# Attention by head pairs: scores on alternating row halves of the array, value products as unsplit float32 on its column halves

## The chip, the core and the metric

The kernel runs on one core of a Trainium2 chip. The metric is device time in microseconds (us), the median of three runs. The engines are named as in the profile: PE is TensorE's matmul, PEld its weight load, DVE is VectorE, ACT is ScalarE, POOL is GpSimd, SP is SyncE.

## The reference

Two layers of an encoder on 512 tokens of width 1024. A layer normalises its input, projects it, and feeds three head groups: A, six heads of dense latent attention; B, six heads of dilated window attention; C, a state-space layer. Their outputs are normalised, concatenated, projected and added to the input; a gated MLP with a convolution follows. What the change touches are the two attentions, cut here to their core:

```python
def dense_attention(q, k, v):                       # group A, head size 96 for q and k, 64 for v
    sc = einsum("bhqe,bhke->bhqk", qb, k) * e ** -0.5
    p = softmax(sc, axis=-1)
    return einsum("bhqk,bhkd->bhqd", p, v)

def dilated_branch(q, k, v, window, dilation):      # group B, head size 64, three patterns
    sc = where(valid, einsum("bhrnqe,bhrnke->bhrnqk", qb, kb) * e ** -0.5, NEG_INF)
    p = exp(sc - max(sc)); den = sum(p)
    o = einsum("bhrnqk,bhrnke->bhrnqe", p, vb) / den   # branches merged by their denominators
```

## The kernel before, in words

The input projection, the state-space layer, attention, the output projection (tile wo) and the MLP (tiles up and dn) run one after the other, for layer 0 and then layer 1. Products are made in float32r, a form of float32 that the array takes in one pass with less precision; to keep precision an operand is split into a high part (ACT rounds it) and a low part (DVE or POOL subtracts), and a product is three matmuls: high by high, low by high, high by low (`mm3`, L348 to L350). The transposes and the small sums are plain float32.

Attention (in `mixing`, from L995) works in heads, two heads to a pair. Group B's three pairs come first, then group A's three. The two heads of a B pair lie on partitions 0-63 and 64-127 of the same tiles; an A head fills 128 rows. For each head, `scores` makes a 128-query tile against 512 keys by three matmuls into a bank of tag sc: 64 rows of the array for B, 128 for A. `unit` then makes the softmax: DVE scales, adds the mask and takes the minimum (L1068, tile P), ACT takes the exponential (L1070), PE transposes P in four blocks into a bank of tag pt (L1074), ACT copies that as the high part (pth, L1078), and DVE makes the low part (ptl, L1079). After two such tiles, `pv` multiplies them with the values: per block of 128 keys three matmuls of 256 columns (L1086 to L1088), twelve for each head and each half of the queries. All of them write 128 partitions, as the values of a head are padded with 64 columns of zeros (`values`, `vput`, tiles vah, val, vbh, vbl), so that the two heads of a pair add into one bank of tag pv. `finish_pair` divides by the sums.

Between these, other work of the layer is traced at lower priority: queries and keys of later heads (`dil_qk` for B, `mla_qk` for A; the latter queues its root and its key's last steps in `later`, which `catch_up` runs), the gated output of group C (`s5_glu`), the norms of the three groups (`mix_group`) and A's values (`mla_values`). In layer 0, `background` also brings in chunks of the modulation (a load and one long DVE instruction each). A scheduler orders every engine's instructions when the kernel is built: by priority, `low(name)` sets it back or ahead, `after` puts instructions behind another one on the same engine. The order on an engine is then fixed. PSUM has eight banks; in attention three go to side work (ps), one to pv, two to pt, two to sc. Heads of A are made ahead: the queries and keys of head h + 3 are traced after the units of head h, into three sets of buffers (`qk_parts`).

Of the kernel before, what the change touches and what calls it, by code (L numbers as in the profile page):

```python
# [28 lines left out]
MB = (1, 1)  # L29
# [41 lines left out]
def _constants():  # L71
# [44 lines left out]
    # angle per position and sign of the sine  # L116
# [100 lines left out]
def program(ctx, tc, a, out):  # L217
# [9 lines left out]
    # 16 tiles: the normed input in two parts, then group A's latents (0-7) and two pairs of queries and keys (8-15)  # L227
# [147 lines left out]
    def bcast42(r4):  # L375
        """r4 [128 tokens, 4, 2] -> PSUM [128, 512]: the first value on partitions 0-63, the second above."""
# [8 lines left out]
    def row_rsqrt(parts, root=False, nt=4):  # L385
        """parts: (maker of a tile AP [rows, 512] of squares, weight column AP [rows, 1]); -> rsqrt(sum + eps) [128, 4]."""
# [18 lines left out]
    def x_norm(c, first):  # L405
        """1 / root mean square of the tokens c of x, on every partition; first: of the kernel's input."""
# [22 lines left out]
    def scaled(l, which, gname):  # L429
        """gain * (1 + sc) columns and the shift columns of one sub-layer."""  # L430
# [14 lines left out]
    def norm_half(l, which, g, c):  # L445
        """which: 0 before the mixing, 24 before the gated MLP. In steps: squares, sums, broadcast, the normed input."""
# [8 lines left out]
    def step(gen, ins):  # L455
        """the next step of a norm, on the tensor engine behind ins; gives its last instruction there."""
# [9 lines left out]
    def rope_tables():  # L466
# [5 lines left out]
        for tab, f in ((tabA, fr[:, 0:1]), (tabS, fr[:, 3:4])):  # L472
            # the angle less whole turns
# [8 lines left out]
            # cosines as sin(pi/2 - |x|)  # L482
# [33 lines left out]
        # rotation tables exp(i*4*theta*n), n ascending forwards, descending backwards  # L516
# [3 lines left out]
        # powers of the discretised diagonal, exponents -2..2  # L520
# [14 lines left out]
        # (a_bar - 1) / a  # L535
# [212 lines left out]
    def mixing(l, background):  # L748
# [5 lines left out]
        # x normed, shifted and scaled, split in two parts  # L754
# [24 lines left out]
        # input projection  # L779
# [17 lines left out]
        def proj_halves(o):  # L797
            """the first group of columns, its first half in one half of the tokens after the other"""
# [48 lines left out]
        def qk_parts(name, src, par):  # L847
            if par:
                i = 4 + 4 * par + 2 * (name == "k")
                hi, lo = ht(i), ht(i + 1)  # L850
            else:
                hi, lo = (mp.tile([128, N], F32R, tag=f"{name}{x}0", name=name + x) for x in "hl")
# [24 lines left out]
        # group C's channels and group B  # L877
# [52 lines left out]
        # group A latents: their mean squares  # L930
# [8 lines left out]
        # ra: columns (cq, ckv) x 4 token tiles; extra: mean-square share of the rotary key + eps  # L939
# [28 lines left out]
        # the 64 rows that are left: the high part, and the low part under it  # L968
# [5 lines left out]
        # roped key part, on rows 64-95 and again on 96-127  # L974
# [5 lines left out]
        # over the latent's factor, which the keys' common one brings back  # L980
# [16 lines left out]
        banks(f"pb{l}", att, ps=3, pv=1, pt=2, sc=2)  # L997
# [5 lines left out]
        # small weights of group A  # L1003
# [39 lines left out]
        def values(name):  # L1043
            hi = ap.tile([128, 4, 576], F32R, tag="vh", name=name + "h")
            lo = ap.tile([128, 4, 576], F32R, tag="vl", name=name + "l")
            for v in (hi, lo):
                G.memset(as32(v).rearrange("p t (c k) -> p (t c) k", k=192)[:, :, 64:128], 0.0)
            return hi, lo

        def vput(vh, vl, t, src, r):  # L1050
            """src PSUM [128 tokens, 384] (times r per token) into the padded layout, two parts."""
            s6 = src.rearrange("p (c k) -> p c k", k=128)
            h6, l6 = (v[:, t].rearrange("p (c k) -> p c k", k=192) for v in (vh, vl))
            for i in range(2):
                si, o = s6[:, :, i * 64:i * 64 + 64], slice(i * 128, i * 128 + 64)
                S.activation(h6[:, :, o], si, AF.Identity, scale=1.0 if r is None else r)
                if r is None:
                    V.tensor_tensor(l6[:, :, o], si, as32(h6[:, :, o]), sub)
                else:
                    V.scalar_tensor_tensor(l6[:, :, o], si, r, as32(h6[:, :, o]), mul, sub)  # L1060

        zero = zcol.to_broadcast([128, N])

        def unit(S_ps, scale, qt, PT, sums, pre):
            """softmax of one 128-query tile, transposed into PT (two parts); scale: minus the scores' factor."""
# [10 lines left out]
            ph, pl = PT  # L1076
            qc = slice(qt % 2 * 128, qt % 2 * 128 + 128)
            S.copy(ph[:, :, qc], t3)  # L1078
            V.tensor_tensor(pl[:, :, qc], t3, as32(ph[:, :, qc]), sub)  # L1079

        def pv(o, PT, vh, vl, hh, first, last, pr):
            c0 = pr * 192 + hh * 64
            ph, pl = PT
            for k in range(4):
                vhk, vlk = vh[:, k, c0:c0 + 128], vl[:, k, c0:c0 + 128]
                T.matmul(o, vhk, ph[:, k], start=(first and k == 0), stop=False)  # L1086
                T.matmul(o, vlk, ph[:, k], start=False, stop=False)  # L1087
                T.matmul(o, vhk, pl[:, k], start=False, stop=(last and k == 3))  # L1088

        def pt_tiles():  # L1090
            return (ap.tile([128, 4, 256], F32R, tag="pth", name="pth", bufs=2),
                    ap.tile([128, 4, 256], F32R, tag="ptl", name="ptl", bufs=2))
# [9 lines left out]
        def scores(q, k, rows, qt):  # L1102
            o = ps("sc", "sc")
            c = slice(qt * 128, qt * 128 + 128)
            (qh, ql), (kh, kl) = q, k
            T.matmul(o, qh[rows, c], kh[rows], start=True, stop=False)  # L1106
            T.matmul(o, ql[rows, c], kh[rows], start=False, stop=False)  # L1107
            T.matmul(o, qh[rows, c], kl[rows], start=False, stop=True)  # L1108
            return o

        full = slice(0, 128)
# [3 lines left out]
        def mla_qk(h, wq):  # L1115
# [18 lines left out]
            q = qk_parts("q", qf, h % 3)  # L1134
            made = [q, None, None]

            def roots():
# [18 lines left out]
                def rest():  # L1156
# [3 lines left out]
                    made[1] = qk_parts("k", kf, h % 3)  # L1160
# [6 lines left out]
        def mla_values():  # L1167
            wuv = small(a["w_uv"][l], 384, name="wuv")
            vh, vl = values("va")
            for t in range(4):  # L1170
# [5 lines left out]
                vput(vh, vl, t, o[:, :384], ra[:, 4 + t:5 + t])  # L1176
            return vh, vl
# [11 lines left out]
        # group B: the three branches as one softmax with key multiplicities  # L1189
        with low("vb"):  # L1190
          dvh, dvl = values("vb")
          for t in range(4):
            o = ps("vtp")
            for j in range(3):
                T.transpose(o[:, j * 128:(j + 1) * 128], draw[6 + j][:, t * 128:t * 128 + 128], ident)
            vput(dvh, dvl, t, o[:, :384], None)
        for pr in range(3):
            q, k = ahead[pr]
            sums = ap.tile([128, 8], F32, tag="sums", name="sums", bufs=2)
            o = ps("pv", "pv")  # L1200
            for hh in range(2):
                rows = slice(hh * 64, hh * 64 + 64)
                for half in range(2):
                    PT = pt_tiles()
                    for qt in (2 * half, 2 * half + 1):
                        unit(scores(q, k, rows, qt), -0.125, qt, PT,
                             sums[:, hh * 4 + qt:hh * 4 + qt + 1], K("bias", 384 - 128 * qt, 512))
                    with low("pv"):
                        pv(o[:, half * 256:half * 256 + 256], PT, dvh, dvl, hh, hh + half == 0, hh + half == 2, pr)
                    catch_up()  # L1210
                    if pr == 0 and hh == half:
                        with low("dq"):
# [286 lines left out]
```

## Time and profile before

| | us |
|---|---|
| median of 3 runs | 1524.69 (1522.24 to 1528.4) |
| the profiled execution, its span from the first instruction to the last | 1525.1 |
| PE busy in it | 1422.6 (93%) |
| DVE busy | 1092.1 (72%) |
| ACT busy | 721.4 (47%) |
| POOL busy | 380.2 (25%) |

The page gives no other time of the profiled execution than its span; nothing around it is shown. A busy matmul time is a union of modelled durations, which run past the start of the next matmul; how long one really holds the array is seen from the distance between the starts of two that follow each other. An fp32r tile prints as f32 among a matmul's operands, so the type is read from the code. A float32 product that is not a transpose stands as two matmuls in the trace.

### The profile page before, as it was taken

Reading aid. Unit: us, or ns where it says so; the run is one execution under the profiler, and the core shown is the slowest. Engines: PE = TensorE matmul, PEld = TensorE weight load, DVE = VectorE, ACT = ScalarE, POOL = GpSimd, SP = SyncE. Lnnn points to the kernel's source line nnn. Section 1 sums busy time; section 2 is a strip of 40 time slices with the busy share of each in tenths; the row PEclk is TensorE's granted clock in tenths of the full one; section 3 lists DMA queues with packets and bytes.
Section 4 is the critical chain, followed back from the end, with each engine's and each line's share of the span. In section 5 each row is a group of like instructions: output and inputs, shape, how many; then the busy total and the mean of one; then the engine's idle time right before and its main releaser. Section 6 shows DMA issues by size and latency. Waiting matters only on the chain.

```text
span 1525.1 us, 20842 instructions
## 1 busy us (share of the span) xinstructions
PE 1422.6 (93%) x7352; PEld 1177.7 (77%) x7352; DVE 1092.1 (72%) x2189; ACT 721.4 (47%) x1419; POOL 380.2 (25%) x330
## 2 busy tenths in 40 slices
PE   4879789989889999999998979999999999999998
PEld 3658567768878878888888867678898888888887
DVE  7996976886799789788656387758748663664663
ACT  4464265675354434444456324657635442442441
POOL 2566441231122153233233334313202000000000
PEclk9989888899999999999999889989999999999999
DMA  7665312311748467467336342000031333233332
GB/s 252 193 190 183 120 27 76 92 36 51 224 146 262 125 222 249 147 218 241 106 100 198 105 130 65 24 27 10 1 104 61 101 102 100 88 95 106 91 93 98
DMA packets 79115, 185.14 MB, mean 121 GB/s; under 512 B 12705, under 2 KB 37793, under 8 KB 79010
## 3 DMA queue, kind: packets, MB, share of 16 engines
q1 hardware_dynamic: 77712, 181.43, 38.0%
q10 hardware_dynamic: 1298, 2.37, 0.4%
q8 instruction: 58, 0.95, 0.3%
q14 instruction: 47, 0.39, 0.1%
HBM read 165.95 MB, written 15.73 MB: 119 GB/s over the span
## 4 chain that ended last, share of the span: by engine, by line
PE 67%; DVE 11%; ACT 3%; issue 3%; DMA 3%; POOL 2%; DVEq 0%; ACTq 0%; POOLq 0%; SPq 0%
PE up L349 10%; PE up L350 10%; PE up L348 10%; PE dn L350 5%; PE dn L349 5%; PE dn L348 5%; PE pt L1074 2%; PE sc L1106 1%; PE pv L1086 1%; PE pv L1088 1%; PE pv L1087 1%; PE s5y L701 1%; PE sc L1108 1%; PE sc L1107 1%; PE u L349 1%
## 5 line engine op out<-in xcount | busy, mean ns | idle before, releaser
L342 ACT CAST wh<-raw 128x512 fp32r<-128x512 f32 (+3 forms) x400 | 223.2, 567 | 307.3 <-PE dn L350 120.6
L348 PE MATMUL up<-t,wh 128*128 128x512 f32 (+1 forms) x736 | 279.4, 381 | 2.5 <-ACT t L442 2.2
L349 PE MATMUL up<-t,wl 128*128 128x512 f32 (+1 forms) x736 | 279.3, 381 | 1.7 <-DVE wl L343 1.7
L350 PE MATMUL up<-t,wh 128*128 128x512 f32 (+1 forms) x736 | 278.2, 381 | 1.2 <-DVE t L443 1.2
L343 DVE TENSOR_TENSOR wl<-raw,wh 128x512 fp32r<-128x512 f32 (+3 forms) x296 | 200.4, 681 | 101.4 <-ACT wh L342 101.0
L343 POOL TENSOR_TENSOR wl<-raw,wh 128x384 fp32r<-128x384 f32 (+1 forms) x104 | 136.5, 1314 | 280.5 <-ACT wh L342 276.2
L348 PEld LDWEIGHTS up<-t,wh 128*128 128x128 f32 x736 | 138.2, 188 | 30.1 <-ACT t L442 3.7
L349 PEld LDWEIGHTS up<-t,wl 128*128 128x128 f32 x736 | 138.1, 188 | 29.8 <-DVE wl L343 2.8
L350 PEld LDWEIGHTS up<-t,wh 128*128 128x128 f32 x736 | 137.2, 188 | 28.8 <-DVE t L443 2.4
L349 PE MATMUL dn<-gh,wl 128*128 128x512 f32 (+1 forms) x366 | 140.7, 386 | 2.0 <-DVE wl L343 2.0
L348 PE MATMUL dn<-gh,wh 128*128 128x512 f32 (+1 forms) x366 | 141.2, 387 | 0.0
L350 PE MATMUL dn<-gl,wh 128*128 128x512 f32 (+1 forms) x366 | 140.8, 386 | 0.0
L327 DVE CUSTOM_DVE_ANT_0 rawm<-rawm,cact,cols 128x1024 f32<-128x1024 f32 x84 | 115.1, 1372 | 14.3 <-DMA rawm<-in_wmod 13.8
L349 PE MATMUL u<-t,wl 128*128 128x512 f32 (+1 forms) x248 | 99.5, 402 | 7.0 <-POOL wl L343 4.0
L348 PE MATMUL u<-t,wh 128*128 128x512 f32 (+1 forms) x248 | 100.4, 410 | 4.2 <-ACT t L442 2.1
L350 PE MATMUL u<-t,wh 128*128 128x512 f32 (+1 forms) x248 | 97.1, 399 | 4.8 <-DVE t L443 4.5
L1070 ACT ACTIVATE P<-P,nb 128x512 f32<-128x512 f32 x96 | 69.3, 722 | 28.2 <-DVE nb L1068 13.2
L349 PEld LDWEIGHTS dn<-gh,wl 128*128 128x128 f32 x366 | 68.8, 188 | 15.9 <-DVE wl L343 2.8
L348 PEld LDWEIGHTS dn<-gh,wh 128*128 128x128 f32 x366 | 68.8, 188 | 14.4 <-ACT gh L1388 1.1
L1078 ACT CAST pth<-pt 128x512 fp32r<-128x512 f32 x96 | 55.7, 587 | 49.8 <-PE pt L1074 48.9
L350 PEld LDWEIGHTS dn<-gl,wh 128*128 128x128 f32 x366 | 68.5, 188 | 13.8 <-DVE gl L1389 1.3
L1079 DVE TENSOR_TENSOR ptl<-pt,pth 128x512 fp32r<-128x512 f32 x96 | 64.8, 685 | 15.5 <-ACT pth L1078 15.1
(447 smaller groups left out, 3085.3 us busy)
## 6 DMA issues: line engine op xcount, KB each, us to landing
raw<-in_w_up SPq DMA_DIRECT2D x88, 512.0 KB, 3.7
rawm<-in_wmod SPq DMA_DIRECT2D x84, 512.0 KB, 4.5
raw<-in_w_dn SPq DMA_DIRECT2D x32, 448.0 KB, 3.3
raw<-in_w_dn SPq DMA_DIRECT2D x16, 512.0 KB, 3.7
raw<-in_w_in SPq DMA_DIRECT2D x40, 192.0 KB, 2.6
raw<-in_wmod SPq DMA_DIRECT2D x12, 512.0 KB, 3.7
raw<-in_w_in SPq DMA_DIRECT2D x16, 320.0 KB, 3.7
s5wcp<-s5d SPq DMA_DIRECT2D x8, 640.0 KB, 5.4
```

The lines of the kernel that those rows point to most:

```text
L327: V.tensor_tensor_reduce(out=r, in0=r, in1=cact, scale=0.5, scalar=col(l, "bmod", j), op0=mul, op1=add, accum_out=modv[l][:, j:j + 1])
L342: S.copy(hi[:, :n], src)
L343: (eng or V).tensor_tensor(lo[:, :n], src, as32(hi[:, :n]), sub)
L348: T.matmul(o, wh, xh, start=first, stop=False)
L349: T.matmul(o, wl, xh, start=False, stop=False)
L350: return T.matmul(o, wh, xl, start=False, stop=last).ins
L701: T.matmul(y[:, j * 128 + lo:j * 128 + hi], cp[:, ri * 2 + j], vt[:, ri, j, lo:hi], start=False, stop=(j == 1 and d == 1 and ri == 1))
L1070: S.activation(P, P, AF.Exp, scale=-1.0, bias=nb, accum_out=sums)
L1074: T.transpose(t_ps[:, c], P[:, c], ident)
L1078: S.copy(ph[:, :, qc], t3)
L1079: V.tensor_tensor(pl[:, :, qc], t3, as32(ph[:, :, qc]), sub)
L1086: T.matmul(o, vhk, ph[:, k], start=(first and k == 0), stop=False)
```

## The change

- Both heads of a pair are worked at a time: the loop runs over six pairs, the two halves of the queries, the two 128-query tiles of a half, and innermost the two heads.
- For B, `scores2` makes the scores of both heads together: six matmuls, alternating between the upper and the lower 64 rows, into two banks. `after` and a high priority (`together`) keep the six in a row. A's scores stay as they were.
- The values and the transposed probabilities are no longer split. `unit` copies the transposed tile once, as float32: ACT for the first head, DVE for the second. The values lie without padding (384 columns), written by one DVE copy (B) or one ACT instruction (A) per 128 tokens.
- `pv` runs once for a pair and a half of the queries: per block of 128 keys one float32 matmul per head, 64 columns of weights, the second head's into partitions 64-127 of the bank and the first head's into 0-63, in turn, kept together by priority.
- PSUM banks: side work 2 instead of 3, sc 3 instead of 2.
- Side work is handed out by a generator, `side(n)`, two steps for each pair. A's heads 0 and 1 are traced in pair 1, head 2 in pair 2, head 3 in the first half of pair 3, heads 4 and 5 in the first and the second half of pair 4, for use in pair 5. Queries and keys have four sets of buffers instead of three. The modulation chunks come two at a time, once for each half of an A pair, instead of one for each head and half.

```diff
-        banks(f"pb{l}", att, ps=3, pv=1, pt=2, sc=2)
+        banks(f"pb{l}", att, ps=2, pv=1, pt=2, sc=3)
...
-            ph, pl = PT
-            qc = slice(qt % 2 * 128, qt % 2 * 128 + 128)
-            S.copy(ph[:, :, qc], t3)
-            V.tensor_tensor(pl[:, :, qc], t3, as32(ph[:, :, qc]), sub)
-
-        def pv(o, PT, vh, vl, hh, first, last, pr):
-            c0 = pr * 192 + hh * 64
-            ph, pl = PT
+            dst = PT[:, :, qt % 2 * 128:qt % 2 * 128 + 128]
+            if hh:
+                V.tensor_copy(dst, t3)
+            else:
+                S.copy(dst, t3)
+
+        def together(first):
+
+            return ExitStack() if first else tc.high_priority(TOGETHER)
+
+        def pv(o, PT, v, pr, first, last):
+
             for k in range(4):
-                vhk, vlk = vh[:, k, c0:c0 + 128], vl[:, k, c0:c0 + 128]
-                T.matmul(o, vhk, ph[:, k], start=(first and k == 0), stop=False)
-                T.matmul(o, vlk, ph[:, k], start=False, stop=False)
-                T.matmul(o, vhk, pl[:, k], start=False, stop=(last and k == 3))
+                for hh in (1, 0):
+                    c0 = pr * 128 + hh * 64
+                    with together(k == 0 and hh):
+                        T.matmul(o[hh * 64:hh * 64 + 64], v[:, k, c0:c0 + 64], PT[hh][:, k],
+                                 start=(first and k == 0), stop=(last and k == 3))
...
+        def scores2(q, k, qt):
+
+            o = [ps("sc", "sc") for _ in range(2)]
+            c = slice(qt * 128, qt * 128 + 128)
+            e = None
+            for i, (x, y) in enumerate(((q[0], k[0]), (q[1], k[0]), (q[0], k[1]))):
+                for hh in (1, 0):
+                    r = slice(hh * 64, hh * 64 + 64)
+                    with after(*[e] if e else ()), together(not e):
+                        e = T.matmul(o[hh], x[r, c], y[r], start=i == 0, stop=i == 2).ins
+            return o
...
+            elif n == 4:
+                with low("qk"):
+                    ahead.append(next_qk(4))
+                yield
+                with low("qk"):
+                    ahead.append(next_qk(5))
...
+        for n in range(6):
+            pr = n % 3
             sums = ap.tile([128, 8], F32, tag="sums", name="sums", bufs=2)
             o = ps("pv", "pv")
+            beside = side(n)
+            for half in range(2):
+                PT = pt_tiles()
+                for qt in (2 * half, 2 * half + 1):
+                    if n < 3:
+                        S2 = scores2(*ahead[n], qt)
+                    for hh in range(2):
...
+                if n >= 3:
+                    background(2)
+                with low("pv"):
+                    pv(o[:, half * 256:half * 256 + 256], PT, dv if n < 3 else va[0], pr, half == 0, half == 1)
+                catch_up()
+                next(beside)
+                catch_up()
+            catch_up()
```

## Rows read from the trace of the kernel before

**Rows 1.** The page: engines' busy time, and the chain that ended last, by engine.
```profile
PE 1422.6 (93%) x7352; PEld 1177.7 (77%) x7352; DVE 1092.1 (72%) x2189; ACT 721.4 (47%) x1419; POOL 380.2 (25%) x330
...
PE 67%; DVE 11%; ACT 3%; issue 3%; DMA 3%; POOL 2%; DVEq 0%; ACTq 0%; POOLq 0%; SPq 0%
```

**Rows 2.** Busy time by stretch: attention of layer 0, then of layer 1.
```profile
core 0: us, PE busy (x) PEld busy (x) DVE busy (x) ACT busy (x) POOL busy (x), PEclk, DMA share, GB/s
185.00:369.00 184.00, 166.41 (x912) 130.91 (x913) 135.78 (x345) 110.51 (x239) 50.07 (x39) 0.87 0.17 49
950.00:1107.00 157.00, 149.88 (x891) 119.45 (x891) 115.14 (x309) 107.26 (x234) 42.20 (x33) 0.96 0.06 17
```

**Rows 3.** PE's longest waits in attention of layer 0: us in total, times, longest.
```profile
PE sc L1106 <- DVE nb L1068: 7.0, 4, 2.7
PE ssq L391 <- POOL sqk L1027: 2.7, 2, 1.9
```

**Rows 4.** PE's longest wait in attention of layer 1.
```profile
PE sc L1106 <- DVE nb L1068: 2.9, 5, 1.0
```

**Rows 5.** Groups on DVE in layer 1's attention: count, busy us, mean ns, idle before.
```profile
L1079 DVE TENSOR_TENSOR ptl<-pt,pth 128x512 fp32r<-128x512 f32 x48 | 32.3, 684 | 6.4 <-ACT pth L1078 6.2
L1068 DVE CUSTOM_DVE_ANT_0 P<-sc,zcol,qs 128x512 f32<-128x512 f32 x24 | 17.7, 744 | 5.8 <-PE sc L1108 4.4 <-PE pt L1074 1.3
...
L1058 DVE TENSOR_TENSOR vbl<-vtp,vbh 128x192 fp32r<-128x192 f32 x8 | 2.5, 352 | 0.6 <-ACT vbh L1056 0.5
```

**Rows 6.** Groups on ACT in the same stretch.
```profile
L1070 ACT ACTIVATE P<-P,nb 128x512 f32<-128x512 f32 x48 | 34.7, 723 | 13.5 <-DVE nb L1068 7.6 <-DVE hv L1146 2.3 <-DVE rs_th L360 1.7
L1078 ACT CAST pth<-pt 128x512 fp32r<-128x512 f32 x48 | 27.8, 586 | 20.8 <-PE pt L1074 20.1
```

**Rows 7.** PE in order of time, layer 1, group B: start us, length us, instruction.
```profile
950.32 0.39 PE L1107 MATMUL sc<-kh,ql 64*128 64x512 f32 x1
950.55 0.39 PE L1108 MATMUL sc<-kl,qh 64*128 64x512 f32 x1
950.79 0.39 PE L1106 MATMUL sc<-kh,qh 64*128 64x512 f32 x1
...
960.53 0.28 PE L1086 MATMUL pv<-pth,vbh 128*128 128x256 f32 x1
960.65 0.28 PE L1087 MATMUL pv<-pth,vbl 128*128 128x256 f32 x1
...
961.47 0.28 PE L1088 MATMUL pv<-ptl,vbh 128*128 128x256 f32 x1
...
969.91 0.39 PE L1107 MATMUL sc<-kh,ql 64*128 64x512 f32 x1
970.23 0.66 PE L1074 MATMUL pt<-cst,P 128*128 128x128 f32 x4
970.82 0.49 PE L1108 MATMUL sc<-kl,qh 64*128 64x512 f32 x1
971.25 0.66 PE L1074 MATMUL pt<-cst,P 128*128 128x128 f32 x4
```

**Rows 8.** The float32 product of L978: ns min/median/max; it stands as two matmuls per layer.
```profile
L978 PE MATMUL krp<-sqd,cst x4: 589/874/1187, 176.4 to 947.1; 64*128 64x512 f32 x4
```

**Rows 9.** Score matmuls (float32r): ns min/median/max, forms.
```profile
L1106 PE MATMUL sc<-t,t x64: 383/480/793, 215.8 to 1096.9; 64*128 64x512 f32 x32, 128*128 128x512 f32 x32
```

**Rows 10.** Weight loads of the value products.
```profile
L1086 PEld LDWEIGHTS pv<-pth,vah x96: 186/188/192, 294.1 to 1105.6; 128*128 128x128 f32 x96
```

**Rows 11.** PE in order of time: the last query product of A's head 5, layer 1.
```profile
1079.91 0.50 PE L1121 MATMUL qps<-t,sml 64*128 64x512 f32 x1
```

**Rows 12.** POOL in order of time: the low part of that head's keys.
```profile
1087.63 1.30 POOL L854 TENSOR_TENSOR t<-glg,t 128x512 fp32r<-128x512 f32 x1 [3.48 <-ACT t L853]
```

More of the change, by code (lines that the diff above doesn't have):

```diff
@@ L845, in dil_done, with qk_parts @@
             V.tensor_scalar(dss[:, j:j + 8], so[:, :8], EPS, None, op0=add)
[L847 to L849 removed]
+        def qk_parts(name, src, n):
+            if n % 4 in (1, 2):
+                i = 4 + 4 * (n % 4) + 2 * (name == "k")
                 hi, lo = ht(i), ht(i + 1)
             else:
[L852 removed]
+                hi, lo = ((ap if n % 4 else mp).tile([128, N], F32R, tag=f"{name}{x}{n % 4}", name=name + x)
+                          for x in "hl")
             S.copy(hi, src)
@@ L1043, in values, with unit @@
         def values(name):
[L1044 to L1060, printed above, removed]
+            return ap.tile([128, 4, 384], F32, tag="v", name=name, bufs=2)
         zero = zcol.to_broadcast([128, N])
-        def unit(S_ps, scale, qt, PT, sums, pre):
+        def unit(S_ps, scale, qt, hh, PT, sums, pre):
             P = ap.tile([128, N], F32, tag="P", name="P", bufs=2)
@@ L1100, in finish_pair, with scores @@
             V.tensor_tensor(dst, o, rb, mul)
-        def scores(q, k, rows, qt):
+        def scores(q, k, qt):
             o = ps("sc", "sc")
             c = slice(qt * 128, qt * 128 + 128)
[L1105 to L1108, printed above, removed]
-            return o
-        full = slice(0, 128)
+            mm3(o, (q[0][:, c], q[1][:, c]), k, True, True)
+            return o
+        def scores2(q, k, qt):
[8 more added lines that the diff above has]
+            return o
         rks = [None]
@@ L1190, in mixing @@
         with low("vb"):
[L1191 to L1198, printed above, removed]
+            dv = values("vb")
+            for t in range(4):
+                o = ps("vtp")
+                for j in range(3):
+                    T.transpose(o[:, j * 128:(j + 1) * 128], draw[6 + j][:, t * 128:t * 128 + 128], ident)
+                V.tensor_copy(dv[:, t], o[:, :384])
@@ new lines, in side @@
+        def side(n):
+            if n == 0:
+                for _ in range(2):
+                    with low("dq"):
+                        ahead.append(dil_qk(len(ahead)))
+                    yield
+            elif n == 1:
+                with low("qk"):
+                    ahead.append(next_qk(0))
+                with low("glu"):
+                    s5_glu(l, mp, oc)
+                yield
+                with low("qk"):
+                    ahead.append(next_qk(1))
+            elif n == 2:
+                with low("mc"):
+                    mix_group("mc", [oc[:, 0], oc[:, 1]], 6, (6, 7, 8, 9))
+                yield
+                with low("va"):
+                    va.append(mla_values())
+                with low("qk"):
+                    ahead.append(next_qk(2))
+            elif n == 3:
+                with low("qk"):
+                    ahead.append(next_qk(3))
+                yield
+                with low("mb"):
+                    mix_group("mb", ob, 3, range(6))
+            elif n == 4:
+                with low("qk"):
+                    ahead.append(next_qk(4))
+                yield
+                with low("qk"):
+                    ahead.append(next_qk(5))
+            while True:
+                yield
@@ L1199, in mixing @@
+        va = []
+        for n in range(6):
+            pr = n % 3
             sums = ap.tile([128, 8], F32, tag="sums", name="sums", bufs=2)
             o = ps("pv", "pv")
[L1201 to L1212, printed above, removed]
-                            ahead.append(dil_qk(len(ahead)))
-                if hh == 0 and pr == 1:
-                    with low("glu"):
-                        s5_glu(l, mp, oc)
-                elif hh == 0 and pr == 2:
-                    with low("mc"):
-                        mix_group("mc", [oc[:, 0], oc[:, 1]], 6, (6, 7, 8, 9))
@@ L1252, in mixing @@
+            catch_up()
+            if n >= 3:
+                oa[pr] = ap.tile([128, N], F32, tag=f"ob{pr}", name=f"oa{pr}")
+            with low("fin"):
+                finish_pair(o, sums, (oa if n >= 3 else ob)[pr])
         ocr = mp.tile([128, 2, N], F32R, tag="oc", name="ocr")
```

51 lines of the change are left out of this document (13 added, 38 removed).

## The prediction

> **What bounds the kernel now.** I read the page first, for the engine that sets the end: PE is busy 93% of the span and holds 67% of the chain [rows 1]. Then the stretches: the change touches attention alone, 184.0 us in layer 0 and 157.0 in layer 1, so at most 341.0 of 1525.1 us are in play. There PE is busy 166.4 and 149.9 us, DVE 135.8 and 115.1, ACT 110.5 and 107.3 [rows 2]. Then PE's waits: its longest kind is 7.0 us in layer 0 and 2.9 in layer 1 [rows 3, 4]. So PE does not stand still for others; it is full. What a matmul holds it for is read from starts, not durations: value products start 0.12 us apart (960.53 to 961.47 are eight steps, 0.1175 each), 512-column scores 0.23 apart, on 64 rows too, as long as the form stays the same (950.55, 950.79) [rows 7]. Where the form changes, a step is longer: from a 64-row score to the transposes 0.32 instead of 0.23 (969.91 to 970.23), and four transposes before such a score 0.59, the score before the next transposes 0.43 [rows 7]. I count 0.1 us for each change of form.
>
> One more thing is to be seen: the granted clock is 0.87 in layer 0 and 0.96 in layer 1 [rows 2]. With levels 1 and 0.5 this means (1 - 0.87) / 0.5 = 26% of 184.0, 48 us, at 1.2 GHz in layer 0, and 13 us in layer 1.
>
> The sum is made against the profiled span, 1525.1 us; the median of the runs, 1524.69, is 0.4 below it, so no correction is made.
>
> **Value products.** There are 24 groups (two layers, six pairs, two halves of the queries). Before, a group is two heads by twelve matmuls: 24 x 0.1175 = 2.82 us. After, it is eight float32 products. A float32 product is two matmuls, and each streams its columns twice: 512 columns on 64 rows take 589 ns at the least where float32r takes 383 [rows 8, 9], 206 more, one more passage of 512 columns. So a group is 16 matmuls of 256 columns, each as long on the array as a float32r one of 512, 0.23 us. One after another that is 3.68 us, 0.86 more than before. If the two column halves run side by side, the order of issue sets the gain: the two matmuls of the second head, then the two of the first. The second matmul of a product can lie beside the first of the next, which is the other head's, and nothing else can; 16 matmuls then take 9 slots, 2.07 us, 0.75 less. No row shows column halves. Ends: 24 x 0.86 = +21 us, and 24 x -0.75 = -18. I take -18, since the nearest row, the value products of today, follow each other in 0.12 us although each has a load of 188 ns of its own [rows 7, 10]: the array already takes the next operand while it streams, and a half that stands idle is more than that asks for. The Trainium skill, TensorE: Matmul & The Clock Gate, Part 3 (Measured speedup vs the span model), states a speedup of 2.38 for three column tiles, 0.79 of the ideal. At that, two halves would make a group 3.68 / 1.59 = 2.3 us, and the gain 6 us smaller, an estimate from that page; no run here shows it.
>
> **Fewer changes of form.** In rows 7's stretch the twelve matmuls of a call are cut in two pieces by scores or transposes, about four edges a call. With 48 calls at 0.1 us that is 19 us. After, 24 groups held together have two edges each; at 0.1 to 0.2 us these are 5 to 10. I take -10 (ends -14 and 0, the latter if the groups are cut after all).
>
> **B's scores.** There are 48 tiles of three matmuls, 144 in all. Steps run from 0.23 in a row to 0.43 at an edge [rows 7]; at a mean of 0.30, nearer to the row, 43 us. After, 24 groups of six: side by side 3 x 0.23, with two edges 0.89 us, 21 in all, so -22. If the row halves don't overlap, 6 x 0.23 + 0.2 = 1.58, 38 in all, -5. I take -22. A's scores are unchanged; a third bank for them lets one more wait finished, which costs nothing.
>
> **DVE and ACT.** Gone are 48 low parts per layer, 32.3 us on DVE in layer 1 [rows 5]; added are 24 copies of the same size. No row shows that copy on DVE; ACT's takes 586 ns [rows 6], DVE's subtraction from the same bank 684 [rows 5]; ends 0.3 (half of ACT's) and 0.69, and I take 0.65. DVE: -32.3 + 15.6, -17 per layer, and about -1 for the values (eight low parts of 352 ns gone, four copies added). ACT: -24 x 0.586 = -14 per layer. PE was the full engine, so this is not added to the sum; it is what lets PE's gain through. Afterwards layer 1 has some 98 us on DVE and 90 on ACT beside 125 to 130 of PE's. POOL loses its four fills of zeros per layer, and they were beside other work.
>
> **What is handed back.** (a) The queries and keys of A's last two heads are now made in pair 4 and used in pair 5, where before a head had three heads of time. For head 5, the last query product starts at 1079.91 and the low part of its keys ends at 1087.63 + 1.30 = 1088.93, 9 us [rows 11, 12]. Its side step stands behind the last units of pair 4; what PE can do meanwhile is that pair's value group, its division and the first head's scores, some 4 us, and an earlier start if the order allows it. Behind a stalled score stand all later transposes and value groups. Ends 0 and 6 us per layer; I take 1.5, since PE's longest waits of today are for the softmax and not for a head's key [rows 3, 4]. (b) One bank less for side work, and modulation chunks two at a time: with DVE freer, between 0 and 3 us per layer; I take 1. (c) With PE 15% shorter, the softmax chain of a tile (0.74 + 0.72 us on DVE and ACT, transposes, a copy of 0.6 to 0.7 [rows 5, 6]) is next to be late. Two buffers of P allow a tile each 1.2 us or so, and PE needs about 2.7, so it costs only where a group of six scores or sixteen value matmuls bunches; I take 10% of PE's gain, 5 us.
>
> **The sum.** PE -18 - 10 - 22 = -50. Handed back 2 x 1.5 + 2 x 1 + 5 = 10. Net -40; from 1525.1 that is 1485. In layer 0 the low clock stretches some of what is removed (a matmul at 1.2 GHz costs double, and 26% of the stage is there), 24 us x 0.26 = 6 at most; I count half, and forecast 1482.
>
> **Rivals.**
> *The columns do not overlap.* Then the value products cost +21 instead of -18. For it: no row with column halves, and float32 is another path than float32r. Against: the streams of successive matmuls already follow seamlessly. Time: 1482 + 39 = 1521; no change that can be measured.
> *The weight loads come out into the open (slower than before).* If a load for one column half cannot be hidden while the other half streams, all 16 matmuls of a group pay their load: up to 188 ns each [rows 10], 16 x (0.23 + 0.19) = 6.7 us a group against 2.07 in the forecast, +111, time about 1593. It decides early: the break-even is a group of 2.07 + 43 / 24 = 3.86 us, that is a serial one (3.68) with 11 ns of each load in the open. Against: loads of full width are hidden in steps of 0.12 us [rows 7, 10]. The Trainium skill, TensorE: Matmul & The Clock Gate, Part 3 (The mechanism), states just such a rule: a load overlaps running matmuls only where the row group differs, and column halves share all rows. The full-width steps in this trace do not follow it; no row shows halves.
> *The clock or the softmax chain takes half of it.* PE has fewer columns in the same stage; if layer 1 fell to layer 0's 0.87, then of some 130 us 34 would be at 1.2 GHz instead of 13, +10 us, and the same again with the tight hand-over at its upper end (2 x 4.5): 1482 + 20 = 1502. For it: DVE's idle time before the softmax is already put down to PE in both directions [rows 5]. Against: DVE and ACT lose 17 and 14 us per layer.
> *More is gained.* In layer 0 DVE is at 74%, with long modulation steps; if relief there also lifts the low clock, that stage falls by up to 24 us more (48 us at half speed, done in 24): 1458.
>
> **How the numbers follow.** Chances: forecast (1465 to 1493) 0.54, clock or chain (1493 to 1512) 0.17, more (below 1465) 0.11, columns serial (1512 to 1530) 0.12, loads in the open (above 1533) 0.06. The range 1452 to 1518 holds the forecast, the chain, most of the larger gain and a part of the serial case. Half a per cent, 7.6 us, is about what a measurement of this kernel can tell from no change. Faster by more than that (below 1517): 0.54 + 0.17 + 0.11 = 0.82, a little more from the serial case's lower edge less a little from the chain's tail: 0.82. Within: 0.11. Slower: 0.07.
>
> **What would show it.** Starts in a value group: two matmuls of different heads within a few ns of each other and 0.23 us between the pairs if the columns overlap; even steps of 0.23 if not; over 0.3 if loads are in the open. Six scores in about 0.7 us between their edges. Attention near 130 us in layer 1 and 155 in layer 0. DVE some 17 us lighter per layer. A wait of PE for a head's key (POOL, L854's counterpart) at the start of pair 5 would show the hand-over. The prediction is wrong if PE's waits for DVE or ACT in attention grow by more than 15 us, or if the granted clock falls below 0.87 in layer 1.

## The result and the profile after

The changed kernel takes 1506.24 us (median of four runs, 1498.45 to 1508.42) against 1523.47 (1517.94 to 1528.4): a ratio of 0.9881, 95% interval 0.9846 to 0.9916. Run again later beside other kernels it had 1501.30 us and 0.9846 (0.9809 to 0.9883). By these ratios it is 18 to 23 us faster. The forecast was 1482, a gain of 43: the direction was right, and between two fifths and a little over half of the size came. The profiled execution took 1506.77 us with a span of 1505.0; the 1.8 us around the span my sum had left out.

The page after, as in [rows 1]:
```profile
PE 1385.0 (92%) x7160; PEld 1116.8 (74%) x7160; DVE 1070.4 (71%) x2117; ACT 693.3 (46%) x1347; POOL 373.0 (25%) x322
...
PE 65%; DVE 19%; DMA 4%; issue 4%; POOL 3%; ACT 3%; SPq 1%; DVEq 0%; ACTq 0%; POOLq 0%
```

PE's share of the chain is nearly the same as before. DVE's went from 11% to 19%, but only in this profile; in a second profile of the same changed kernel (run f1 below) it is 12%, so nothing is built on it:
```profile
PE 66%; DVE 12%; ACT 3%; POOL 3%; DMA 3%; issue 2%; SPq 0%; DVEq 0%; ACTq 0%; POOLq 0%
```

Attention from its first score to its last value product, layer 0 and layer 1, with the columns of [rows 2]:
```profile
193.00:354.00 161.00, 142.65 (x798) 96.03 (x797) 120.21 (x305) 94.29 (x200) 43.26 (x32) 0.88 0.17 54
...
933.00:1086.00 153.00, 137.57 (x795) 95.34 (x794) 102.97 (x273) 93.60 (x199) 40.67 (x31) 0.89 0.06 18
```

Layer 1 is only 4 us shorter, although PE is busy 12 us less, and its granted clock fell from 0.96 to 0.89. In layer 0 the first score comes later in the state-space layer than before, so these edges flatter it. I therefore use a stretch with the same edges in every kernel, from the state-space layer's last product to the first product of the MLP (it takes in the output projection). Before (first two rows) and after (last two):
```profile
191.00:426.00 235.00, 211.17 (x1288) 175.47 (x1288) 174.92 (x435) 131.78 (x286) 62.01 (x52) 0.90 0.29 88
935.00:1156.00 221.00, 212.92 (x1346) 178.27 (x1345) 151.10 (x397) 134.86 (x295) 56.01 (x49) 0.96 0.13 39
```
```profile
192.00:414.00 222.00, 196.07 (x1198) 148.37 (x1198) 161.86 (x399) 116.90 (x250) 56.56 (x47) 0.89 0.30 94
918.00:1136.00 218.00, 198.80 (x1251) 152.78 (x1250) 140.48 (x364) 121.18 (x259) 53.60 (x45) 0.92 0.13 40
```

To see what PE's time was, I took each matmul's hold of the array from the trace (from its start to the next start, or to its end where idle time follows) and multiplied it by the granted clock; that is its work at full clock. The hold minus that is what the low clock cost. In us:

```
stretch   kernel   length  PE work  low clock cost  PE idle | value  scores B  scores A  transposes  side  out-projection
layer 0   before   234.4   187.9    22.7            23.9    | 38.4   19.1      19.9      22.4        40.8  47.3
          after    221.3   172.7    22.7            25.9    | 22.4   14.4      20.2      23.0        45.8  46.8
layer 1   before   221.3   204.3     8.7             8.3    | 38.1   22.6      19.9      22.0        55.4  46.4
          after    218.2   183.4    15.5            19.3    | 22.5   14.3      19.9      22.8        57.3  46.7
```

PE lost 15.2 + 20.9 = 36 us of work. (Six of B's 144 score matmuls start before the stretch in the kernel before, from 185.2 us on; with their 1.4 us B's scores there are 43.1.) Of the 36 us, 16 came through in the two stretches, 13.1 and 3.1. The span fell by 20 because the part between them, where nothing was changed, was 5.1 us shorter: the low clock happened to cost 5.1 there instead of 11.3. What did not come through went into idle time (+2.0 and +11.0) and, in layer 1, the lower clock (+6.8). In f1's profile 18 of 35 us came through, with 15 us more of idle time and 1 of low clock; so the idle time comes back from one profile to the next, and the low clock wanders by some 6 us. What PE waits for in layer 1 is no longer one thing; the longest, as in [rows 4]:
```profile
PE ssq L391 <- POOL sqk L1029: 2.4, 2, 1.3
PE bc L382 <- DVE glv L870: 2.0, 1, 2.0
PE bc L372 <- DVE rks L1150: 1.9, 2, 1.7
...
PE sc L348 <- ACT kh L855: 1.2, 1, 1.2
```

They are links of side work (sums, broadcasts, queries and keys) through POOL, DVE and ACT.

The value groups, in the view of [rows 10]: a load and a matmul.
```profile
L1078 PEld LDWEIGHTS pv<-pt,va x192: 132/137/231, 290.3 to 1084.9; 128*64 128x64 f32 x192
L1078 PE MATMUL pv<-pt,va x192: 379/379/689, 290.3 to 1085.1; 128*64 128x256 f32 x192
```
And PE in order of time in layer 1, as in [rows 7]: B's scores (L1107), transposes, a value group, transposes.
```profile
955.18 1.39 PE L1107 MATMUL sc<-t,t 64*128 64x512 f32 x6
956.62 0.66 PE L1060 MATMUL pt<-cst,P 128*128 128x128 f32 x4
957.20 0.50 PE L1107 MATMUL sc<-t,t 64*128 64x512 f32 x1
957.73 0.66 PE L1060 MATMUL pt<-cst,P 128*128 128x128 f32 x4
958.31 0.96 PE L1107 MATMUL sc<-t,t 64*128 64x512 f32 x5
959.78 1.95 PE L1078 MATMUL pv<-pt,vb 128*64 128x256 f32 x16 [0.51 <-DVE pt L1064]
961.66 0.66 PE L1060 MATMUL pt<-cst,P 128*128 128x128 f32 x4
```

Sixteen matmuls of 379 ns end within 1.95 us, and the next matmul starts 1.88 us after the first: the column halves overlap. Most groups take this long; those at the low clock take up to 3.68. The scores do not come as planned. In 13 of the 24 groups the first matmul goes alone, and transposes stand between it and the other five (957.20 to 958.31); where all six follow each other, as from 955.18, their starts (955.18, 955.61 twice, 955.95 twice, 956.18) show the second head one matmul behind the first, so the first and the last have no partner.

DVE in layer 1, as in [rows 5]:
```profile
L1064 DVE COPY pt<-pt 128x512 f32<-128x512 f32 x24 | 16.5, 688 | 11.8 <-PE pt L1060 11.4
```

### The profile page after: what moved, and what is told of

Same layout as the page of the kernel before. It is cut to its first block, busy times and chain, and to the rows that moved or that the text cites. A ratio compares the mean times of both kernels' runs of the same rounds, so it can differ in the third digit from the quotient of the medians.

```text
span 1505.0 us, 20265 instructions
## 1 busy us (share of the span) xinstructions
PE 1385.0 (92%) x7160; PEld 1116.8 (74%) x7160; DVE 1070.4 (71%) x2117; ACT 693.3 (46%) x1347; POOL 373.0 (25%) x322
## 4 chain that ended last, share of the span: by engine, by line
PE 65%; DVE 19%; DMA 4%; issue 4%; POOL 3%; ACT 3%; SPq 1%; DVEq 0%; ACTq 0%; POOLq 0%
PE up L349 9%; PE up L350 9%; PE up L348 9%; PE dn L350 5%; PE dn L349 5%; PE dn L348 5%; DVE rawm L327 3%; PE pv L1078 3%; PE pt L1060 2%; DMA rawm<-in_wmod 2%; PE wo L348 2%; PE wo L349 1%; PE wo L350 1%; PE u L349 1%; DVE wl L343 1%
## 5 line engine op out<-in xcount | busy, mean ns | idle before, releaser
L350 PEld LDWEIGHTS up<-t,wh 128*128 128x128 f32 x736 | 137.3, 188 | 28.7 <-DVE t L443 2.4
L348 PE MATMUL u<-t,wh 128*128 128x512 f32 (+1 forms) x248 | 97.8, 399 | 4.8 <-ACT t L442 2.6
L350 PE MATMUL u<-t,wh 128*128 128x512 f32 (+1 forms) x248 | 95.6, 393 | 4.2 <-DVE t L443 4.0
L350 PEld LDWEIGHTS dn<-gl,wh 128*128 128x128 f32 x366 | 68.5, 188 | 13.9 <-DVE gl L1400 1.3
L1060 PE MATMUL pt<-cst,P 128*128 128x128 f32 x384 | 63.4, 293 | 4.1 <-ACT P L1056 3.4
L1419 DVE SCALAR_TENSOR_TENSOR xs<-dn,modv,xs 128x512 f32<-128x512 f32 (+1 forms) x50 | 36.2, 727 | 41.3 <-PE dn L350 41.3
```

Of the source, the lines that this page charges most:

```text
L348: T.matmul(o, wh, xh, start=first, stop=False)
L350: return T.matmul(o, wh, xl, start=False, stop=last).ins
L1060: T.transpose(t_ps[:, c], P[:, c], ident)
L1419: return V.scalar_tensor_tensor(xs[:, m, c], o, modv[l][:, 40 + m:41 + m], xs[:, m, c], mul, add).ins
```

## The experiments

Each run is given with its median and its ratio to the kernel before on the same chip, with the 95% interval; the changed kernel's two are 0.9881 and 0.9846, 0.986 in the mean, and 0.001 is 1.5 us. Taken together, the intervals of two kernels leave their difference uncertain by some 5 us for e3, 7 for e5 and e6, 10 for f4 against f1 and 12 for g2 against f4, so the shares below are rough.

**Undoing the overlaps.** In e3 the value products of one head follow those of the other.
```diff
-            for k in range(4):
-                for hh in (1, 0):
+            for hh in (1, 0):
+                for k in range(4):
```


> The changed kernel with the value products of one head after those of the other in each group, so that the column halves cannot overlap; same instructions. Overlap gone: a group of 16 takes 3.6 us instead of 1.88. If PE is the bound throughout (theory 3) the 24 groups cost 24 x 1.75 = +42 us, 1548. If PE has slack in layer 1 by now (theories 1 and 2), about half of layer 1's 21 us goes into waits and low clock that are there anyway: +25 to +33 us, 1531 to 1539.

1516.66 us, 0.9958 (0.9937 to 0.9979). Every engine kept its order: the traces of e3 and of the changed kernel have the same operations one after another on PE, DVE, ACT and POOL. The overlap went only in part, as a group in e3 shows:
```profile
980.38 2.86 PE L1078 MATMUL pv<-pt,vb 128*64 128x256 f32 x16
```
PE's work in the two stretches rose by 11.6 and 10.2 us, 22; by the ratios the kernel is 15 us slower. Work added to PE counts by about two thirds.

In e4 the same was done to B's scores.
```diff
-            for i, (x, y) in enumerate(((q[0], k[0]), (q[1], k[0]), (q[0], k[1]))):
-                for hh in (1, 0):
+            for hh in (1, 0):
+                for i, (x, y) in enumerate(((q[0], k[0]), (q[1], k[0]), (q[0], k[1]))):
```


> The changed kernel with the three scores of one B head after those of the other, so that the row halves cannot overlap; same instructions. A group of six goes from 0.7 to 1.4 us plus edges. PE the bound throughout (theory 3): 24 x 0.68 = +16 us, 1522. Slack by now (theories 1 and 2): +4 to +10 us.

1497.95 us, 0.9831 (0.9784 to 0.9878): not slower with 7 us more of PE work, against every theory. But the scheduler had also given DVE, ACT and PE another order, so this run does not tell of the overlap. e5 takes both heads' scores from the same rows instead, which leaves every engine's order as it was.
```diff
-                    r = slice(hh * 64, hh * 64 + 64)
+                    r = slice(64, 128)
```


> The changed kernel with both heads' scores of B taken from rows 64-127 (head 0's scores are then head 1's): the row halves cannot overlap, and every engine's instructions and their order stay exactly as in the changed kernel, which was not so where the three scores of a head were put in a row (that run was 8 us faster). PE gets some 0.68 us of work more in each of 24 groups, 16 us. Theory A (PE still bounds attention): +16 us, 1522. Theory B (the chain through DVE, ACT and POOL bounds it about half of the time; the run with serial rows was faster by the accident of another order): +4 to +10 us. Theory C (PE's lost streaming time lowers its clock, and more of it keeps the clock up): no change or up to 8 us faster, with less time at 1.2 GHz in layer 1's attention than 34 us.

1517.19 us (1504.62 to 1524.95), 0.9949 (0.9910 to 0.9988): 13 us slower by the ratios for 11.5 us more PE work. The twelve times lie in two groups, six from 1505 to 1513 and six from 1521 to 1525, and the profiled execution (1512.15) is of the lower one; its stretches are 9 us longer than the changed kernel's. So the work that is put back counts for most of its size or in full. Theory C, that more PE work would keep the clock up and cost nothing, falls.

e6 goes the other way and leaves out half of the value products.
```diff
-            for k in range(4):
+            for k in (0, 3):
                 for hh in (1, 0):
```


> The changed kernel with half of the value products left out (two of four key blocks). PE's work falls by 24 x 0.86 = 21 us. The schedule changes too. Theory A (PE bounds): 1485. Theory B (the chain bounds): 1496 to 1506. Theory C (clock): no change or slower.

1497.20 us, 0.9809 (0.9770 to 0.9848): PE's work fell by a further 13.9 + 8.8 = 23 us, the time by 8 by the ratios. So one third counts in this direction. Unlike e3 and e5 this run also changed the order on every engine, so the third is not of PE's work alone. Its stretches, layer 0 and layer 1, have more low clock in layer 0 (0.85):
```profile
190.00:407.00 217.00, 187.14 (x1098) 143.82 (x1098) 158.37 (x399) 115.79 (x250) 56.36 (x47) 0.85 0.31 96
912.00:1126.00 214.00, 187.28 (x1158) 145.33 (x1156) 137.38 (x361) 121.82 (x259) 53.03 (x45) 0.94 0.14 40
```

**Suspects named in the prediction.** e1 makes A's heads 4 and 5 half a pair earlier, with buffers of their own for head 4's queries and keys (not shown).
```diff
                 with low("mb"):
                     mix_group("mb", ob, 3, range(6))
-            elif n == 4:
                 with low("qk"):
                     ahead.append(next_qk(4))
-                yield
+            elif n == 4:
                 with low("qk"):
                     ahead.append(next_qk(5))
```


> The changed kernel with A's head 4 made in the second half of pair 3 and head 5 in the first half of pair 4 (half a pair earlier each), a buffer set of their own for head 4's queries and keys and six buffers for the query factors. Theory 1 (late hand-over: the saved PE work of layer 1 turned into waits behind the chain that makes the next heads, and the clock fell in those waits): the hole between the value groups of pair 4 and pair 5 in layer 1 closes, layer 1's stretch from the state-space layer to the MLP goes from 218 to about 208 us, and the whole to 1490 to 1497 from 1506. Theory 2 (too few banks for side work): no change beyond 4 us, since the number of banks is the same. Theory 3 (PE is still the bound and only the sizes of my terms were off): no change beyond 4 us.

1504.22 us, 0.9879 (0.9842 to 0.9917). Layer 1's stretch fell from 218.2 to 211.0 us in the one profiled execution, but no gain is to be seen in the times. So the tight hand-over is not seen to take the missing time; nor are the banks, in e2:
```diff
-        banks(f"pb{l}", att, ps=2, pv=1, pt=2, sc=3)
+        banks(f"pb{l}", att, ps=3, pv=1, pt=2, sc=2)
```


> The changed kernel with the banks as before: three for side work, two for scores. Theory 2 (too few banks for side work): 8 us or more faster, 1498 or less, PE's waits for sums and broadcasts in attention (L372, L391, L1139, L1141) shrink by half. Theory 1 (late hand-over): within 4 us, or slower by up to 10, as the six scores of a B pair then need both banks empty.

1506.74 us, 0.9896 (0.9852 to 0.9940). Nor the two buffers of P, in e7 (`bufs=2` to `bufs=4`):

> The changed kernel with four buffers for the tile P of the softmax instead of two, so that DVE and ACT can run four tiles ahead of the transposes. Theory B with the softmax as its chain: 5 us or more faster, 1501 or less, with less idle time of PE in attention (19 and 26 us now). Theory B with the side work as its chain, and theories A and C: within 4 us.

1508.69 us, 0.9880 (0.9838 to 0.9922). e8 joined e1 and e4:

> Both edits that were faster so far: the scores of one B head after those of the other, and A's heads 4 and 5 made half a pair earlier. If both gains are of a cause of their own they add: 8 + 2, 1496. If they are accidents of the schedule: anywhere from 1490 to 1510.

1509.15 us, 0.9898 (0.9864 to 0.9931): nothing adds, so no gain of either is shown. These edits also made the scheduler order all engines anew; each answer is for the edit together with the order that it got.

**Work on the other engines.** e9 sets the value groups back (`"pv": 30` in `PRI`):

> The changed kernel with the value groups set back by 30 in priority, so that scores and transposes of the next tiles go ahead of them on PE. Theory S (attention waits for the chain of the softmax, scores to DVE to ACT to transposes, and a block of 1.9 us on PE in its way delays it): 5 us or more faster, 1501 or less. Theory Q (it waits for the chain that makes queries and keys) and theory M (only the order's accidents differ): within 5 us.

1497.94 us, 0.9840 (0.9778 to 0.9901). e10 puts both copies on ACT:
```diff
-            if hh:
-                V.tensor_copy(dst, t3)
-            else:
-                S.copy(dst, t3)
+            S.copy(dst, t3)
```


> The changed kernel with both heads' copies of the transposed tile on ACT: DVE loses 16.5 us per layer, ACT gains 14. If DVE's load is what attention waits for: 6 us or more faster, 1500 or less. If the two engines' loads don't matter but the chain does (theories S and Q): within 5 us. If ACT becomes the bound: slower by 5 or more.

1494.04 us, 0.9819 (0.9754 to 0.9884). e12 makes the low parts of queries and keys on DVE instead of POOL (in `qk_parts`, `G.tensor_tensor` to `V.tensor_tensor`):

> The changed kernel with the low parts of queries and keys (18 a layer, 1.3 us each on POOL) made by DVE in about 0.7. Theory Q (the chain that makes queries and keys): 5 us or more faster, 1501 or less, as each link of that chain is 0.6 us shorter. Theories S and M: within 5 us, or slower since DVE is loaded more.

1496.83 us, 0.9839 (0.9785 to 0.9893). Each of the three is a little better than the changed kernel, but none by more than the intervals allow. e11 takes the modulation chunks out of layer 0's attention (the two lines with `background(2)` there are gone):

> The changed kernel with layer 0's twelve modulation chunks taken out of attention; they follow in the output projection and its end. DVE loses 15 us in layer 0's attention and gets them in the stretch behind it. If DVE bounds layer 0's attention: the stretch of attention shrinks by 8 or more, and the whole by 0 to 8. If not: within 4 us, or slower by up to 15 where nothing hides the chunks behind.

1526.18 us, 1.0032 (1.0002 to 1.0063). Nothing hides them behind attention: the output weights are loaded in the same stretch as the chunks, and ACT waits 38.1 us for them (14.3 in the changed kernel), then PE for ACT:
```profile
ACT wh L342 <- DMA raw<-in_w_out: 38.1, 2, 31.4
PE wo L348 <- ACT wh L342: 28.2, 2, 27.7
```
Attention itself did not gain. In layer 0, from the state-space layer's last product to behind the last value product, DVE is 14 us lighter in e11 (second row) than in the changed kernel (first row), but the last value product ends 158.7 us after that product, against 161.2 and, in f1, 159.0. So DVE's load alone does not bound layer 0's attention.
```profile
192.00:354.00 162.00, 143.65 (x802) 97.03 (x802) 120.21 (x305) 94.79 (x201) 43.26 (x32) 0.88 0.17 54
191.00:353.00 162.00, 142.01 (x823) 99.61 (x823) 106.41 (x286) 95.17 (x203) 42.24 (x32) 0.91 0.05 15
```

f1 is the changed kernel again (numbers above), and f2 swaps which head's copy is on which engine (`if hh` to `if not hh`), so that loads stay and only order differs.

> The changed kernel once more, beside the next three on the same chip: 1506, between 1498 and 1509 as before.

> The changed kernel with head 0's copies of the transposed tile on DVE and head 1's on ACT: every engine has the same work, only the order differs. Theory M (the gains of 8 to 12 us are accidents of order, which the changed kernel happens to have badly): 1494 to 1500, as with those edits. Theory D (DVE's load is the cause): within 4 us of the changed kernel.

f2: 1502.63 us, 0.9847 (0.9805 to 0.9889), the same as f1: this other order with the same loads gives nothing. f3 joins e10 and e12, f4 adds e9.

> Both copies on ACT and the low parts of queries and keys on DVE instead of POOL. Theory D plus theory Q (DVE's load and the chain over POOL are two causes): the gains of 12 and 9 add in part, 1485 to 1490. Theory D alone: DVE gets back 12 of the 16 us per layer, so about 1497. Theory M: anywhere from 1492 to 1508.

> As the one before, with the value groups set back by 30 in priority too. If these are three causes: 1480 to 1488. Theory M: anywhere from 1492 to 1508.

f3: 1485.95 us, 0.9752 (0.9702 to 0.9802). f4: 1474.05 us, 0.9669 (0.9611 to 0.9726), which beats both kernels, the changed one by 27 us. Its order differs from the changed kernel's too; but e1, e2, e4, e7, e8, e9 and f2 also have other orders of the same operations on PE, and they lie between 0.9831 and 0.9898. Order alone has nowhere given as much. Its PE work in the stretches is 170.0 + 184.8 us, 3 less than f1's 173.7 + 183.8; the two stretches are 203.7 and 209.1 us long instead of f1's 219.3 and 218.1. f4's stretches:
```profile
188.00:392.00 204.00, 183.15 (x1196) 143.30 (x1195) 148.24 (x392) 126.86 (x275) 34.72 (x31) 0.93 0.34 103
897.00:1106.00 209.00, 194.14 (x1258) 149.64 (x1256) 127.63 (x346) 132.35 (x284) 33.51 (x30) 0.95 0.14 42
```
Against the changed kernel DVE is 13 to 14 us lighter in each, POOL 20 to 22, ACT 10 to 11 heavier, and the clock is at 0.93 and 0.95 instead of 0.89 and 0.92. PE's longest waits in its layer 1 are now for the softmax, no longer for links of side work:
```profile
PE pt L1060 <- ACT P L1056: 4.3, 5, 2.3
PE sc L348 <- DVE nb L1054: 2.4, 2, 1.6
PE pv L1075 <- ACT pt L1063: 1.8, 2, 1.4
PE ssq L391 <- POOL sqk L1029: 0.8, 1, 0.8
```

**The two ends.** g1 makes the two of these edits that apply to the kernel before (`"pv": 30`, low parts on DVE).

> The kernel before with the low parts of queries and keys on DVE instead of POOL and the value products set back by 30 in priority (the third edit has no counterpart, its low parts have no copy to move). If PE was its bound, as the forecast has it: within 5 us of it, or slower by the load on DVE. If the chains off PE held it already: 8 to 20 us faster.

1548.99 us, 1.0167 (1.0119 to 1.0214): slower. That the chains off PE held the kernel before in a way that these edits relieve is not seen; the edits load DVE, which still had the 48 low parts of a layer, and the value products are cut more (their hold rose from 76.5 to 85.3 us). Most of the loss stands in the profile as low clock (table below). The reasons for the 25 us are not separated.

g2 is f4 with e3's edit.

> The changed kernel with the three edits (1474 us), and the value products of one head after those of the other, 22 us of PE work more; DVE and ACT keep their order. If PE's work counts for more once the other engines are lighter: 16 to 22 us slower, 1490 to 1496. If it still counts by half: 8 to 12 us slower, 1482 to 1486.

1487.60 us, 0.9781 (0.9729 to 0.9832): 13.6 us by the medians, 17 by the ratios, for 21.9 us of PE work: 62 to 78%, about as in the changed kernel, and again with every engine's order as it was in f4. Lightening the others has moved the level; PE still shares the bound.

Where the time of these edits went in the two stretches together, in us, one profile each (the changed kernel's is its first):

```
run   against          length   PE work   low clock   PE idle
e3    changed kernel   +12.7    +21.9      -6.0        -3.2
e5    changed kernel    +9.4    +11.5      -0.7        -1.5
e6    changed kernel    -8.5    -22.7      +2.8       +11.5
f4    f1               -24.6     -2.7     -10.0       -11.8
g2    f4               +14.1    +21.8      -6.0        -1.8
g1    kernel before    +30.0    +10.6     +18.0        +1.3
f1    changed kernel    -2.2     +1.4      -5.9        +2.3
```

The last row is the same kernel twice: a low clock of 6 us more or less says nothing. Work put back finds little idle time to fill (e3, e5, g2); work taken away mostly opens idle time (e6).

## Why the prediction was wrong

**Value products: right.** A group takes 1.88 us (2.07 forecast), since the halves run abreast from the first matmul on: eight slots, not nine. The limit that I took from the order of issue did not hold, nor did the 2.3 us estimated from three column tiles. With fewer cuts their hold fell from 76.5 to 44.9 us, 32 against 18 + 10. The rivals with serial columns and with loads in the open are out: the sixteen loads of 137 ns in a group are hidden. The sentence of the Trainium skill, TensorE: Matmul & The Clock Gate, Part 3 (The mechanism), that a load overlaps running matmuls only where the row group differs, is not what this trace shows for column halves.

**B's scores: the size was wrong.** The term was -22, from 43 to 21; their hold fell from 43.1 to 28.7 us, -14. I had six in a row with two edges, 0.89 us; a group takes 28.7 / 24 = 1.2, as its first matmul goes alone and in 13 of 24 groups is cut off by transposes.

**Left out of the sum.** Transposes (+1.4) and side work (+6.9) hold PE longer than before, though they are the same work. I charged changes of form to scores and value groups alone; an edge also lengthens the step of the neighbour. That is reasoned from where the holds rose, no run isolates it. Together PE's work in the stretches fell by 36 us instead of 50.

**The step that failed most: "So PE does not stand still for others; it is full", and with it "I take 10% of PE's gain".** Of 36 us, 16 came through in the stretches (18 of 35 in f1). PE's idle time there rose by 13 us (15 in f1) and the low clock's cost by 7 (1 in f1). Work put back counted by two thirds or more (e3: 15 us for 22, e5: 13 for 11.5), work taken away by a third (e6: 8 for 23, with another order): PE is close to the bound, but does not stand alone. I had read the longest kinds of wait, 7.0 and 2.9 us; all of PE's idle time in layer 0's stretch was 23.9 us already before (table above). That the waits were short [rows 3, 4] showed only that PE had something else to do, often side work; that this work had time to spare is my reading and not measured. The chain of the page gave no warning: PE's 67% [rows 1] is also what f4 has, where PE is busy 93% as before:
```profile
PE 67%; DVE 12%; DMA 3%; ACT 3%; issue 2%; POOL 2%; SPq 0%; DVEq 0%; ACTq 0%; POOLq 0%
```

I named the softmax chain as next to be late; e7 found no gain from more tiles of it in flight. Two copies moved to ACT, the low parts moved from POOL to DVE and the later place of the value groups together gave 27 us (f4), with PE's work unchanged: the engines beside PE, and the order in which they serve it, held that much. How these 27 us split between DVE's load, the chain over POOL, the priority and the order that came with them is open; singly each is within the intervals, and DVE's load alone gave nothing in layer 0 (e11).

**The rival that came nearest** is "The clock or the softmax chain takes half of it", 1493 to 1512: the time fell there, its causes only in part. It took 10 us from a lower clock in layer 1 and 9 from the hand-over. Layer 1's granted clock did fall (0.96 to 0.89 in attention), which cost 6.8 us in one profile and 5.6 in f1; more PE work did not lift it (e5 has 0.91 in both stretches). Why it fell is open: f2 and e1 have as much idle time in layer 1 (20.0 and 18.4 us) as the changed kernel (19.3), and 5.2 and 8.5 us of low clock instead of 15.5. The signs that I had set, waits grown by more than 15 us or a clock below 0.87, did not come in the first profile, although the gain was halved; they were set too wide.

**The small items.** DVE's copy took 688 ns, at the upper end of 0.3 to 0.69. DVE became 21.7 us lighter on the page (1092.1 to 1070.4), 11 a layer and not 17 or 18. The hand-over of the last heads shows as PE's wait for a key at the start of pair 5, 1.2 us in layer 1 (the wait for kh above) and 2.1 in layer 0, where I took 1.5. In e1 that wait is gone from layer 1.
```profile
PE sc L348 <- ACT kh L855: 2.1, 1, 2.1
```

## What to carry to other kernels

Here the busiest engine was busy 93% of the time, with short waits, and about half of a cut in its work came through, not 90%. Before such a cut is priced in full, price the engines beside it for the shorter stage too, and look for the edits that relieve them in the same change. Read a second profile of the same kernel before a share of the chain or a granted clock is used as evidence. A test of overlap should leave every engine's order unchanged (other data, not other order); a reordering of the schedule by itself can hide the effect that is looked for.

## What the hardware showed that was not expected

Float32 matmuls on the two column halves start together. In this stretch of the changed kernel four matmuls, each two passages of 256 columns long, start in two pairs, 0.007 us apart within a pair and 0.27 us from pair to pair, and are done in 0.65 us:
```profile
978.73 0.65 PE L1078 MATMUL pv<-pt,vb 128*64 128x256 f32 x4
```
And one half need not wait for the other. In e3 the code puts eight matmuls of one head before eight of the other. The trace shows two rows of eight starts, 0.22 to 0.27 us apart in each; it does not name the heads, so that a row is a head is read from the code. The second row begins at 981.30, while three of the first were still to start (981.51, 981.73, 981.94); that is why e3's group took 2.86 us and not 3.5.
